# One transfer a pair for the operand and the result of the triangular inverses, GLA sample values read from 16 copies, and a host order that counts eight transfers under way

## The chip, the cores and the metric

One core of a Trainium2 chip runs the whole program. The core has a tensor engine for matrix products (PE; PEld is its weight load), a vector engine (DVE), a scalar engine (ACT), a general engine (POOL) and a sync engine (SP) that here issues every transfer between the chip's memory and the on-chip buffers (SBUF). Products land in PSUM banks. The metric is the device time of one execution in microseconds; lower is better.

## The reference

One step of a decoder layer for 1024 prompt tokens and 8 sample tokens, model width 1024, all in fp32. The weights are the same for both groups.

```python
p = jnp.einsum('btd,dn->btn', x, w_in)                 # 1024 -> 9360 columns
# GLA, 4 heads: S_t = diag(a_t) S_{t-1} + k_t^T v_t ; o_t = q_t S_t
# RWKV-7, 16 heads of 64:
#   S_t = S_{t-1} (diag(w_t) - kk_t^T (kk_t * a_t)) + v_t^T k_t ; y_t = S_t r_t
m = (jax.nn.sigmoid(gate_a) * jnp.einsum('btc,cd->btd', o_gla, w_up_gla)
     + jax.nn.sigmoid(gate_b) * jnp.einsum('btc,cd->btd', o_rwkv, w_up_rwkv))
out = jnp.einsum('btd,de->bte', m, w_out)
y_out = _layernorm(DEEPNORM_ALPHA * x + out, ln_g, ln_b, LN_EPS)
```

The outputs are the layer's result for both groups and the new states of both recurrences.

## The kernel before

**Passes.** The tokens go through in two passes of 512; the first carries the 8 sample tokens as well. In each pass the input projection runs in blocks of 128 output columns. A block is 24 products for each piece of tokens: eight slices of the model width, and three products each, because weights and tokens are split into a high and a low part (`wpart`, `xh`, `xl`) and the product of the two low parts is left out. The blocks come in a fixed plan (`make_plan`): for each of eight pairs of RWKV heads the rows r, k, v and the output gate, between them the rows of the four GLA heads, and then as many blocks of the merge gates as the list `GATES` gives to that pair. After both passes come the two up projections, the output projection and the normalization.

**A pair of RWKV heads.** `front` makes decays and products for 8 chunks of 64 tokens. Each chunk and head needs the inverse of a 64x64 unit triangular matrix. Its two 32x32 diagonal blocks are inverted on POOL, in 31 steps of a multiply (`Xt`) and an add (`X`). For that the blocks go through the chip's memory: four stores write them to `LD`; four loads of 128 KB (line 1281) bring the same 32 partitions' worth of operand into each quarter of the partitions of `L_` (tile `wide`), since each quarter q holds every fourth column group of the inverses. After POOL, four stores of 32 KB (line 1303) write the inverses from `X` to `XD`, and loads bring them back as `XT` and `Yd`. `back` then transposes a part of `XT` on DVE into `Xd` and forms the off-diagonal block with two small groups of products on PE (`Xd` by `Ld`, then `Yd` by `Xt`). `turn`, `chain` (eight dependent steps of three products on the bank `pch`) and `norm` follow. The buffers of a pair come back when its chain has ended.

**GLA samples.** For each of the four heads `gla_sample` stores the eight sample rows of values to `vd` (line 1040), and for two sample tokens at a time loads them into all 128 partitions (line 1049), next to the state of those tokens.

**The order.** Work is written as generators, one a stream. On the host, `run` keeps a clock for each engine and always emits the operation with the smallest key: its start by the clocks, less a priority of its kind (`PRIO`, for PE `FOR_PE`). Each engine then runs its list strictly in that order; operations that two engines can do go to the one that ends first by these clocks (`start`). A transfer is priced by `transfer` from its packets; the clock `dma` is one queue for all transfers. `AGE` weighs changes of ACT's function table, `BIAS` and `ASIDE` the choice between engines, `URGENT` the weights when PE has none ahead. `AHEAD` is how many blocks ahead the loads of the next tokens' operand (x) start, `RAWS` how many rows of it may be loaded ahead of their casts.

SP issues transfers one after another. The framework gives the transfers a small ring of semaphores: each transfer reuses the one of the transfer eight before it, and SP waits until that one has landed.

Of the kernel before, what the change touches and what calls it, by code (L numbers as in the profile page):

```python
# [10 lines left out]
F32 = mybir.dt.float32  # L11
# [9 lines left out]
P = 128  # L21
# [3 lines left out]
NS = 8  # L25
# [4 lines left out]
GH, GDK, GDV = 4, 128, 256  # L30
# [25 lines left out]
BANKS = {"proj": 2, "big": 5, "pch": 1}  # L56

KEEP = 0
AHEAD = 6

RAWS = 5


WARM = 9
# [3 lines left out]
LEAD = 2  # L68
SPARE_ROWS = 10
EARLY_GATES = 16  # L70
GATES = [[3, 1, 3, 1, 2, 3, 2, 1], [2, 1, 3, 5, 0, 1, 4, 0]]


HOP = {"P": 0.2, "D": 0.418, "G": 0.115, "V": 0.064, "A": 0.14}

AFTER = {"A": 0.13, "V": 0.13, "G": 0.147, "S": 0.13}
SWITCH = 0.092
HOLD = 0.11
TABLE = 1.28

AGE = 1.487

SPARE = 0.411
LANDED = 0.648
BIAS = 0.148
ASIDE = 1.497

PRIO = {"evacuate": 0.383, "pair": 0.309, "turn": 0.598, "chain": 0.413, "norm": 0.266, "x": 0.754,
        "lora": 0.377, "rank": 1.051, "head": 0.246, "gate": -0.174, "w": 0.3, "out": 0.424, "state": 0.186,
        "block": 0.718}  # L90
FOR_PE = {"pair": 1.47, "turn": 1.208, "chain": 0.733, "norm": 1.48, "lora": 1.838, "rank": 2.757,
          "head": 0.983, "gate": 2.698, "state": 2.188, "out": 0}
STAND, SCARCE, PER_ROW = 0.033, 0.043, 0.107

URGENT = 1.952
SIGMOID, EXP = "sigmoid_and_others", "natural_log_exp_and_others"
SETS = {AF.Sigmoid: SIGMOID, AF.Tanh: SIGMOID, AF.Exp: EXP, AF.Ln: EXP}

# [119 lines left out]
def transfer(out, src):  # L218

    n = 4 * min(run_of(out), run_of(src), 512 if src.tensor.space == out.tensor.space else 1024)  # L220
    packets = out.nbytes() / n
    slow = 2.2 if any(int(s) == 0 and int(m) > 1 for s, m in src.ap) else 1.45 if packets <= 32 and n > 2048 else 1.0
    if out.tensor.space == DRAM:
        return packets * (0.01 + n * 4.2e-5) / 16, 1.2
    return slow * packets * (0.01 + n * 4.65e-5) / 16, 1.7
# [46 lines left out]
class Order:  # L272
# [4 lines left out]
    def __init__(self, nc):  # L277
        self.P, self.A, self.V, self.G, self.S, self.E, self.C = (Engine(**e) for e in (
            {"P": nc.tensor}, {"A": nc.scalar}, {"V": nc.vector}, {"G": nc.gpsimd}, {"S": nc.sync},
            {"V": nc.vector, "G": nc.gpsimd}, {"A": nc.scalar, "V": nc.vector}))  # L280
        self.tiles = (P, P)
        self.quads = {"V": {}, "A": {}}
        self.time = dict.fromkeys("PAVGS", 0.0)
        self.port = dict.fromkeys("VG", 0.0)
        self.dma = 0.0
        self.table = EXP
        self.ready, self.read = {}, {}
        self.streams = []
        self.idle, self.make, self.home, self.wait = {}, {}, {}, {}
        self.kept, self.tile = {}, {}  # L290
# [65 lines left out]
    def start(self, op):  # L356

        best = None
        for eng, fn, cost in op.ways:
            free, t = self.time[eng] + (SWITCH if eng == "P" and op.tiles != self.tiles else 0.0), 0.0  # L360
            for x in (*op.outs, *op.ins):
                at, by = self.ready.get(x.tensor.name, (0.0, None))
                if eng == "S" and by == "D" and x is op.out:
                    continue
                if by != eng:
                    at += HOP.get(by, 0.0) + (SPARE if eng == "P" and by in ("V", "A", "G") else LANDED if by == "D" else 0.0)
                elif eng != "P" and x is not op.out:
                    at += AFTER[eng]
                t = max(t, at)
            t = max(t, *(self.read.get(x.tensor.name, 0.0) for x in (*op.outs, *(y for y in op.ins if y.space == PSUM))))  # L370
            if eng in op.port:
                free = max(free, self.port["G" if eng == "V" else "V"])
            late, t = free - t, max(t, free)
            if eng in "VA" and self.held(eng, op):
                cost += HOLD
            end = t + cost
            if len(op.ways) > 1:
                end += BIAS if eng == "V" and "A" in op.ways[0][0] else ASIDE if eng == "G" and "G" in op.port else 0.0
            if best is None or end < best[0]:
                best = end, t  # L380
                op.eng, op.fn, op.cost, op.late = eng, fn, cost, max(0.0, late)
        return best[1]
# [10 lines left out]
    def run(self):  # L393
        while self.streams:
            best, before = None, list(self.streams)
            self.urgent = self.needed()
            stand = max(STAND, SCARCE - PER_ROW * len(self.idle["row"]))
            for s in before:
                self.advance(s)
                if s.op is not None:  # L400
                    t = self.start(s.op)
                    if s.op.eng == "P":
                        key = t - stand * s.for_pe - (SWITCH if s.op.tiles != self.tiles else 0.0)
                    else:
                        key = t - s.prio
                    if s.kind in self.urgent:
                        key -= URGENT
                    if s.op.table not in (None, self.table):
                        key += max(0.0, TABLE - AGE * s.op.late)
                    if best is None or key < best[0]:  # L410
                        best = key, t, s
            if best is None:
                assert self.streams != before, "streams wait for one another"
                continue
            _, t, s = best
            op, s.op = s.op, None
            cost = op.cost
            if op.table not in (None, self.table):
                cost += TABLE
                self.table = op.table  # L420
                self.nc.scalar.preload_act_table_set(self.table)  # L421
            op.fn()
            self.time[op.eng] = max(self.time[op.eng], t + cost)
            if op.eng in op.port:
                self.port[op.eng] = t + cost
            if op.eng == "P":
                self.tiles = op.tiles
            elif op.eng in "VA":
                for x, q in self.starts(op):
                    self.quads[op.eng][x is op.out, x.space] = q  # L430
            end = t + cost
            if op.eng == "S":
                self.dma = max(self.dma, end) + op.lag[0]
                end = self.dma + op.lag[1]
            for x in op.outs:
                n = x.tensor.name
                self.ready[n] = max(end, self.ready.get(n, (0.0,))[0]), "D" if op.eng == "S" else op.eng
            for x in op.ins:
                n = x.tensor.name
                self.read[n] = max(self.read.get(n, 0.0), end)  # L440


class Kern(Order):
# [586 lines left out]
    def gla_sample(self, h, q, k, v, al, bufs):  # L1030
# [5 lines left out]
        vs = vs_[:NS]  # L1036
        yield A.copy(vs, pv_)
        self.free(pv_)
        vd = self.dr.tile([NS, GDV], F32, name=f"vd{h}")
        yield self.S.dma_start(vd, vs)  # L1040
        self.free(vs_)
        W = 2

        def load(n):
            Sg, vb = bufs[n % 2]
            b = slice(n * W, n * W + W)
            yield self.S.dma_start(Sg[:, :W * GDV].rearrange("p (b v) -> p b v", b=W),
                                   a["state_gla"][0, b, h].rearrange("b k v -> k b v"))
            yield self.S.dma_start(vb[:, :W * GDV], vd[b].rearrange("b v -> (b v)").partition_broadcast(P))
        yield from load(0)  # L1050
        yield from load(1)
        po = yield from self.bank("big", [P, 2, GDV])
# [1 line left out]
        for g in range(2):  # L1054
            for n in (2 * g, 2 * g + 1):
                Sg, vb = (x[:, :W * GDV].rearrange("p (b v) -> p b v", b=W) for x in bufs[n % 2])
                for w in range(W):
                    t = HT + n * W + w
# [129 lines left out]
    def front(self, c, p, st, d):  # L1188
        a, A, V, E = self.a, self.A, self.V, self.E
        BK_, L_ = yield from self.get("wide", 2)  # L1190
# [14 lines left out]
        r, kb, v = (x[:, :HT] for x in st)  # L1205
# [51 lines left out]
        for n, y in enumerate(p4):  # L1257
            x, h = H * (n // 2), n % 2
# [3 lines left out]
        NU = 4 * NCH  # L1262
        LD = self.dr.tile([4, NCH, 32, 32], F32, name=f"LD{c.i}{p}")
        for q in range(2):
            b = slice(32 * q, 32 * q + 32)
# [4 lines left out]
        for h in range(2):  # L1270
            for n in range(2):
                g = 2 * h + n
# [3 lines left out]
        X = X_.rearrange("p (i t) -> p i t", t=32)  # L1276
        yield E.memset(X, 0.0)
        for q in range(4):
            yield E.memset(X_[NU * q:NU * q + NU, q::36], 1.0)
        for q in range(4):  # L1280
            yield self.S.dma_start(L_[NU * q:NU * q + NU, :32 * 32], LD.rearrange("n c s t -> (n c) (s t)"))
        BT = self.dr.tile([P, NCH * P], F32, name=f"BT{c.i}{p}")
        for f in range(2):
            y = yield from self.row(HT)
# [5 lines left out]
        for j in range(31):  # L1290
# [5 lines left out]
            if j % 5 == 4 and j < 20:  # L1296
                b = j // 5
# [1 line left out]
        self.free(tm)  # L1299
        XT = (yield from self.get("XT")).rearrange("p (c h t) -> p c h t", c=NCH, h=2)  # L1300
        XD = self.dr.tile([4 * NCH, 32, 32], F32, name=f"XD{c.i}{p}")
        for q in range(4):
            yield self.S.dma_start(XD.rearrange("u (i g) t -> g u i t", g=4)[q], X[NU * q:NU * q + NU])
        self.free(X_)

        Yd_ = yield from self.get("Yd")
# [603 lines left out]
```

## Time and profile before

| | us |
|---|---|
| median of 3 runs | 1439.07 (1438.75 to 1439.47) |
| the profiled execution | 1439.84 |
| its span, first to last instruction | 1438.0 |
| PE busy | 1420.8 |
| DVE busy | 1054.8 |
| ACT busy | 834.2 |
| POOL busy | 412.6 |

In the profile, "out<-in" names what an instruction writes and reads by the program's tiles; nearly every instruction has line 239, the line of the helper that emits it, so tiles tell the places. "x8" counts instructions of a group. Idle time has behind it what ended it. SPq is the sync engine's queue of transfer issues.

### The profile page before, as it was taken

How to read it: one execution, taken by the hardware profiler on the slowest of the kernel's cores; microseconds unless marked ns; L12 is line 12 of the kernel's file. 1: busy time of each engine (PE TensorE's matmuls, PEld its weight loads, DVE VectorE, ACT ScalarE, POOL GpSimd, SP SyncE). 2: the span in 40 equal slices, each digit the busy share in tenths (PEclk: the TensorE clock that was granted, in tenths of full speed). 3: DMA queues.
4: the chain of work that ended last, by engine and by line, in shares of the span. 5: the costliest groups of instructions: out<-in, count | busy, mean ns of one | idle time of the engine just before them, and what ended most of it. 6: DMA issues, size and time to landing. Idle time of an engine off the chain costs nothing.

```text
span 1438.0 us, 30397 instructions
## 1 busy us (share of the span) xinstructions
PE 1420.8 (99%) x10640; PEld 1250.2 (87%) x10640; DVE 1054.8 (73%) x2137; ACT 834.2 (58%) x2074; POOL 412.6 (29%) x1148
## 2 busy tenths in 40 slices
PE   9999999999999999999999999999999999999997
PEld 9999999999999998787878787887888898897786
DVE  6778566978586988558665978889867865666685
ACT  6656757666758675546455646565657664654210
POOL 1050506260525251533414352253423150000000
PEclk9999999999999999999999999999999999999999
DMA  9896889686888786886688677567578578699832
GB/s 323 267 299 204 283 287 312 218 299 224 281 276 279 268 263 210 244 250 180 187 241 253 189 197 228 172 188 249 151 233 238 175 223 264 210 293 318 279 123 84
DMA packets 284788, 340.12 MB, mean 237 GB/s; under 512 B 159027, under 2 KB 174524, under 8 KB 284636
## 3 DMA queue, kind: packets, MB, share of 16 engines
q1 hardware_dynamic: 284636, 338.18, 75.2%
q8 instruction: 85, 1.39, 0.4%
q14 instruction: 67, 0.55, 0.1%
HBM read 210.03 MB, written 127.00 MB: 234 GB/s over the span
## 4 chain that ended last, share of the span: by engine, by line
PE 81%; DVE 7%; ACT 4%; DMA 3%; issue 2%; POOL 2%; SPq 1%; DVEq 0%; ACTq 0%; POOLq 0%
PE proj L239 52%; PE big L239 24%; PE pch L239 5%; DVE row L239 3%; ACT row L239 3%; SPq L239 1%; DVE wide L239 1%; DVE gg L239 1%; POOL Xt L239 1%; POOL X L239 1%; DMA row<-o_rwkv 1%; DVE wpart L239 1%; ACT L421 1%; ACT wpart L239 1%; DMA XT<-XD 0%
## 5 line engine op out<-in xcount | busy, mean ns | idle before, releaser
L239 PE MATMUL proj<-xh,wpart 128*128 128x256 f32 (+3 forms) x3712 | 905.3, 328 | 2.9 <-DVE wpart L239 1.4
L239 PEld LDWEIGHTS proj<-xh,wpart 128*128 128x128 f32 x3712 | 618.5, 188 | 56.3 <-issue 7.3
L239 PE MATMUL proj<-xl,wpart 128*128 128x512 f32 (+3 forms) x1856 | 606.7, 327 | 0.0
L239 PEld LDWEIGHTS proj<-xl,wpart 128*128 128x128 f32 x1856 | 349.7, 188 | 25.1 <-issue 3.1
L239 POOL TENSOR_TENSOR Xt<-X,wide 128x60 f32<-128x60 f32 (+24 forms) x496 | 172.0, 347 | 399.5 <-DMA wide<-LD 292.9
L239 DVE TENSOR_TENSOR wpart<-wraw,wpart 128x512 fp32r<-128x512 f32 x210 | 145.5, 700 | 68.5 <-ACT wpart L239 63.7
L239 POOL TENSOR_TENSOR X<-X,Xt 128x60 f32<-128x60 f32 (+24 forms) x496 | 179.4, 362 | 38.5
L239 DVE TENSOR_TENSOR row<-row 128x512 f32<-128x512 f32 (+9 forms) x340 | 173.5, 525 | 13.6 <-ACT row L239 6.8
L239 ACT CAST wpart<-wraw 128x512 fp32r<-128x512 f32 x210 | 128.8, 619 | 84.4 <-PE proj L239 39.0
L239 ACT ACTIVATE row<-row 128x512 f32<-128x512 f32 (+5 forms) x229 | 137.9, 611 | 6.5 <-DVE row L239 2.7
L239 PE MATMUL big<-xh,wpart 128*128 128x256 f32 (+3 forms) x560 | 132.5, 324 | 0.3 <-ACT xh L239 0.3
L239 POOL TENSOR_TENSOR row<-row 128x512 f32<-128x512 f32 (+3 forms) x29 | 37.5, 1302 | 279.4 <-DVE row L239 162.1
L239 ACT COPY row<-big 64x256 f32<-64x256 f32 (+6 forms) x188 | 63.4, 350 | 73.0 <-PE big L239 67.1
L239 DVE TENSOR_TENSOR wide<-pch,gg 64x65 f32<-64x65 f32 x224 | 49.8, 222 | 75.4 <-PE pch L239 73.0
L239 PEld LDWEIGHTS big<-xh,wpart 128*128 128x128 f32 x560 | 93.5, 189 | 8.4 <-ACT xh L239 0.8
L239 ACT COPY rh<-pch 128x130 f32<-128x130 f32 x125 | 33.5, 268 | 103.9 <-PE pch L239 103.3
L239 PE MATMUL big<-xl,wpart 128*128 128x256 f32 (+3 forms) x280 | 90.2, 322 | 0.5 <-DVE xl L239 0.5
L239 DVE SCALAR_TENSOR_TENSOR row<-proj,pv,row 128x255 f32<-128x255 f32 (+1 forms) x95 | 54.5, 574 | 44.1 <-ACT tail L239 26.1
L239 ACT COPY wide<-pch 64x65 f32<-64x65 f32 x237 | 49.3, 208 | 48.9 <-PE pch L239 45.7
L421 ACT ACT_TABLE_LOAD x60 | 77.0, 1283 | 1.0
L239 PE MATMUL big<-row 128*64 128x64 f32 (+5 forms) x680 | 68.6, 287 | 0.3 <-ACT row L239 0.3
L239 ACT ACTIVATE row<-proj,omu 128x256 f32<-128x256 f32 (+1 forms) x95 | 51.7, 545 | 24.7 <-PE proj L239 23.9
(219 smaller groups left out, 2035.4 us busy)
## 6 DMA issues: line engine op xcount, KB each, us to landing
w<-wpart SPq DMA_DIRECT2D x146, 512.0 KB
wpart<-w SPq DMA_DIRECT2D x146, 512.0 KB
wraw<-w_in SPq DMA_DIRECT2D x146, 256.0 KB
wide<-LD SPq DMA_DIRECT2D x64, 128.0 KB
BT<-row SPq DMA_DIRECT2D x32, 256.0 KB
wide<-BT SPq DMA_DIRECT2D x64, 128.0 KB
wraw<-w_up_gla SPq DMA_DIRECT2D x32, 256.0 KB
row<-w_out SPq DMA_DIRECT2D x32, 256.0 KB
```

Of the source, the lines that this page charges most:

```text
L239: ways.append((eng, lambda call=call: call(out, *args, **kw), price(eng, name, out, args, ins)))
L421: self.nc.scalar.preload_act_table_set(self.table)
```

## The change

The operand of the inverses is loaded by one transfer that reads `LD` four times over, and the inverses are stored by one transfer. The sample values are stored to `vd` sixteen times, and each load reads each copy into eight partitions. In the host's order a transfer may not start before the eighth transfer back has ended by the clocks, less 0.3 us; a repeated source counts as slow only above eight repeats. Eight numbers of the order, two tables of weights and the dealing of the gate blocks are new.

```diff
-AHEAD = 6
+AHEAD = 4
-RAWS = 5
+RAWS = 6
-GATES = [[3, 1, 3, 1, 2, 3, 2, 1], [2, 1, 3, 5, 0, 1, 4, 0]]
+GATES = [[4, 1, 2, 0, 1, 4, 4, 0], [3, 0, 3, 6, 0, 1, 3, 0]]
+FLIGHT, EARLY = 8, 0.3
-AGE = 1.487
+AGE = 1.077
-BIAS = 0.148
-ASIDE = 1.497
+BIAS = 0.149
+ASIDE = 1.951
-PRIO = {"evacuate": 0.383, "pair": 0.309, "turn": 0.598, "chain": 0.413, "norm": 0.266, "x": 0.754,
-        "lora": 0.377, "rank": 1.051, "head": 0.246, "gate": -0.174, "w": 0.3, "out": 0.424, "state": 0.186,
-        "block": 0.718}
-FOR_PE = {"pair": 1.47, "turn": 1.208, "chain": 0.733, "norm": 1.48, "lora": 1.838, "rank": 2.757,
-          "head": 0.983, "gate": 2.698, "state": 2.188, "out": 0}
-STAND, SCARCE, PER_ROW = 0.033, 0.043, 0.107
-URGENT = 1.952
+PRIO = {"evacuate": 0.383, "pair": 0.309, "turn": 0.53, "chain": 0.3, "norm": 0.242, "x": 0.645,
+        "lora": 0.207, "rank": 0.674, "head": 0.199, "gate": 0.131, "w": 0.3, "out": 0.52, "state": 0.151,
+        "block": 1.599}
+FOR_PE = {"pair": 1.84, "turn": 1.151, "chain": 0.476, "norm": 1.207, "lora": 3.885, "rank": 2.504,
+          "head": 0.199, "gate": 2.37, "state": 1.781, "out": 0.03}
+STAND, SCARCE, PER_ROW = 0.013, 0.026, 0.104
+URGENT = 2.707
...
-    slow = 2.2 if any(int(s) == 0 and int(m) > 1 for s, m in src.ap) else 1.45 if packets <= 32 and n > 2048 else 1.0
+    slow = 2.2 if any(int(s) == 0 and int(m) > 8 for s, m in src.ap) else 1.45 if packets <= 32 and n > 2048 else 1.0
...
+        self.flight = [0.0] * FLIGHT
...
+            if eng == "S":
+                t = max(t, self.flight[-FLIGHT])
...
                 end = self.dma + op.lag[1]
+                self.flight.append(end - EARLY)
...
-        vd = self.dr.tile([NS, GDV], F32, name=f"vd{h}")
-        yield self.S.dma_start(vd, vs)
+        vd = self.dr.tile([16, NS * GDV], F32, name=f"vd{h}")
+        yield self.S.dma_start(vd.rearrange("c (b v) -> b c v", b=NS), vs.unsqueeze(1).to_broadcast([NS, 16, GDV]))
...
-            yield self.S.dma_start(vb[:, :W * GDV], vd[b].rearrange("b v -> (b v)").partition_broadcast(P))
+            yield self.S.dma_start(vb[:, :W * GDV],
+                                   vd[:, n * W * GDV:(n + 1) * W * GDV].unsqueeze(0).to_broadcast([P // 16, 16, W * GDV]))
...
-        for q in range(4):
-            yield self.S.dma_start(L_[NU * q:NU * q + NU, :32 * 32], LD.rearrange("n c s t -> (n c) (s t)"))
+        yield self.S.dma_start(L_[:, :32 * 32],
+                               LD.rearrange("n c s t -> (n c) (s t)").unsqueeze(0).to_broadcast([4, NU, 32 * 32]))
...
-        for q in range(4):
-            yield self.S.dma_start(XD.rearrange("u (i g) t -> g u i t", g=4)[q], X[NU * q:NU * q + NU])
+        yield self.S.dma_start(XD.rearrange("u (i g) t -> g u i t", g=4), X)
```

## The prediction

> **What bounds the kernel now.** I read the page first, then the busy time by stretch, then what TensorE waited for, then one such wait in the order of time. From the page: the span, the engines, the chain that ended last, and one of the two groups of the 32x32 inverses on POOL.
>
> ```profile
> span 1438.0 us, 30397 instructions
> PE 1420.8 (99%) x10640; PEld 1250.2 (87%) x10640; DVE 1054.8 (73%) x2137; ACT 834.2 (58%) x2074; POOL 412.6 (29%) x1148
> PE 81%; DVE 7%; ACT 4%; DMA 3%; issue 2%; POOL 2%; SPq 1%; DVEq 0%; ACTq 0%; POOLq 0%
> L239 POOL TENSOR_TENSOR Xt<-X,wide 128x60 f32<-128x60 f32 (+24 forms) x496 | 172.0, 347 | 399.5 <-DMA wide<-LD 292.9
> ```
>
> TensorE (PE) is busy for 1420.8 of 1438.0 us and carries 81% of the last chain. It is idle for 17.2 us in all. POOL waits 292.9 us for the load that this change merges, but POOL is busy only 29% of the span, and most of that wait is POOL standing ready long before the next pair of heads arrives. A big wait on a spare engine is not a big gain. The next view gives the busy time in some stretches (columns: stretch, length, then PE, PEld, DVE, ACT, POOL, clock, DMA share, GB/s).
>
> ```profile
> 108.00:180.00 72.00, 70.60 (x647) 68.52 (x646) 48.69 (x95) 47.84 (x126) 22.48 (x71) 1.00 0.78 245
> 252.00:324.00 72.00, 69.20 (x666) 66.52 (x665) 59.59 (x125) 50.03 (x130) 29.80 (x76) 1.00 0.78 257
> 396.00:468.00 72.00, 70.70 (x647) 67.83 (x646) 52.25 (x103) 50.23 (x129) 26.20 (x73) 1.00 0.84 275
> 1430.40:1438.00 7.60, 0.04 (x1) 0.00 (x0) 4.38 (x9) 0.50 (x2) 0.00 (x0) 0.70 0.19 69
> ```
>
> The last 7.6 us are the end of the program: PE has finished, DVE normalizes the last rows and they are stored. The three stretches, all in the first pass over the tokens, lose 1.4, 2.8 and 1.3 us, 5.5 together. What ended PE's waits (columns: total us, times, longest):
>
> ```profile
> PE pch L239 <- DVE wide L239: 1.8, 4, 1.2
> PE proj L239 <- DVE wpart L239: 1.4, 1, 1.4
> PE proj L239 <- DVE row L239: 1.3, 1, 1.3
> PE pch L544 <- DVE warm L541: 1.1, 1, 1.1
> PE big L239 <- ACT part L239: 0.9, 1, 0.9
> ```
>
> 1.1 us is the start, before the first warm-up product. So 17.2 - 7.6 - 1.1 = 8.5 us is idle time in the middle, in single waits of at most 1.4 us behind DVE or ACT. None names a transfer, but one hides one. Around 296 us the timeline (start, length, engine, what, idle before it) shows:
>
> ```profile
> 294.75 0.62 ACT L239 CAST wpart<-wraw 128x512 fp32r<-128x512 f32 x1 [1.65 <-DMA w<-wpart]
> 295.40 0.69 DVE L239 TENSOR_TENSOR wpart<-wraw,wpart 128x512 fp32r<-128x512 f32 x1 [2.22 <-ACT wpart L239]
> 295.96 0.62 ACT L239 CAST wpart<-wraw 128x512 fp32r<-128x512 f32 x1 [0.59 <-DMA w<-wpart]
> 296.61 0.46 PE L239 MATMUL pch<-wide,gg 128*128 128x130 f32 x2 [1.19 <-DVE wide L239]
> ```
>
> ACT stands for 1.65 us until the store of a weight block has landed and its buffer is free; DVE has the subtraction of that block ahead of the state update, and PE waits 1.19 us for the update. Here the host-written order had expected a transfer sooner than it came.
>
> **The change, part by part.** No product on PE is added or dropped, so the 1420.8 us stay, apart from what a new sequence of shapes does. Three costs remain: SP's issues, the length of the inverse's way through the queues, and the order itself.
>
> *Issues.* Issue times on SP (min/median/max ns):
>
> ```profile
> L239 SPq DMA_DIRECT2D wide<-LD x64: 303/421/916, 63.9 to 1141.9; - x64
> L239 SPq DMA_DIRECT2D XD<-X x64: 549/607/1572, 99.1 to 1182.1; - x64
> SPq L239 <- PE proj L239: 183.9, 96, 5.6
> ```
>
> Each of the 16 pairs loses three loads and three stores: 3 x 0.421 + 3 x 0.607 = 3.1 us of SP, 49 us over the kernel. SP waits 183.9 us for PE alone (buffers that matmuls still read), so this mostly turns into more waiting: worth nothing by itself. It also frees six of the places that the new order counts.
>
> *The operand's load.* The first pair, in order of time:
>
> ```profile
> 63.90 1.85 SPq L239 DMA_DIRECT2D wide<-LD  x4
> 68.22 0.33 POOL L239 TENSOR_TENSOR Xt<-X,wide 128x31 f32<-128x31 f32 x1 [63.24 <-DMA wide<-LD]
> 96.43 0.21 POOL L239 TENSOR_TENSOR X<-X,Xt 128x8 f32<-128x8 f32 x1
> 99.08 0.58 SPq L239 DMA_DIRECT2D XD<-X  x1
> 108.49 0.83 SPq L239 DMA_DIRECT2D XT<-XD  x2
> 111.29 0.93 SPq L239 DMA_DIRECT2D XT<-XD  x2
> 119.11 1.24 DVE L239 STREAM_TRANSPOSE Xd<-XT 32x128 f32<-32x128 f32 x4
> 120.63 0.43 PE L239 MATMUL big<-Xd,Ld 128*32 128x128 f32 x8
> 63.90:68.20 4.30, 4.30 (x38) 4.30 (x38) 2.46 (x4) 4.11 (x10) 0.00 (x0) 1.00 0.77 221
> ```
>
> From the first issue to POOL's start are 68.22 - 63.90 = 4.3 us. In that stretch (last row) the engines were 77% busy at 221 GB/s, so all sixteen would move 221 / 0.77 = 287 GB/s. A 128 KB load needs 0.46 us of data; from the end of the last issue (65.75) to POOL's start are 2.47 us, so about 2.0 us are landing. One load of 512 KB: 0.42 issue + 2.0 landing + 1.83 data = 4.25 us if it spreads over all sixteen engines, a gain of 0.1. No row shows how a copy with only four copies outermost is spread; if it ran on four engines its data would take 4 x 1.83 = 7.3 us and the whole 9.7, a loss of 5.4.
>
> *The store of the inverse.* It saves 1.8 us of issues; its 128 KB take 0.46 us at that rate, or 1.8 on four engines, so it comes out between -1.8 and -0.4 us. The 128-byte pieces may go slower than that rate; the same factor would then lie on both sides. Load and store together move the inverse's result by -1.9 to +5.0 us.
>
> What covers that? In the first pair POOL ends at 96.64 and the store is issued at 99.08, 2.4 us later; the last read-back is issued by 112.22, and with 2.5 us of landing is there at 114.7, while DVE takes it up at 119.11, 4.4 us later. Slack 6.8 us. The tightest case I looked at is the seventh pair:
>
> ```profile
> 525.02 0.27 POOL L239 TENSOR_TENSOR X<-X,Xt 128x8 f32<-128x8 f32 x1
> 525.32 3.51 SPq L239 DMA_DIRECT2D XD<-X  x4
> 533.77 0.92 SPq L239 DMA_DIRECT2D XT<-XD  x2
> 542.36 0.94 DVE L239 STREAM_TRANSPOSE Xd<-XT 32x128 f32<-32x128 f32 x3
> ```
>
> There POOL's end and the store touch, and 534.69 + 2.5 to 542.36 leaves 5.2 us. So slack of 5.2 to 6.8 us, PE's filler of projection blocks meanwhile, covers both ends in the slots of before; I charge 0. Without that cover the next to be late would be the product on Xd (at 120.63, 0.3 us behind its transposes), and behind it everything in PE's queue.
>
> The Trainium skill ("DMA: Bandwidth & Descriptors", section "Why a DMA increments its semaphore by 16 and not by 1") says a copy runs on the largest number of engines up to sixteen that divides the slowest dimension of both its sides, and "Rules for kernel authors" on that page names a leading repeat of c copies as confining it to c. By that rule load and store run on four engines and the slow ends hold; no run here shows it yet. It is a rule against this change, and its result is the second rival.
>
> *GLA values.* The store of the eight sample rows grows from 8 to 128 KB, four times in the kernel: 0.4 us more data at 287 GB/s on sixteen engines, 1.8 if on four. The loads read the same amount.
>
> ```profile
> ACT row L239 <- DMA row<-vd: 0.7, 1, 0.7
> ```
>
> ACT waited 0.7 us for them in all, while PE ran blocks: 0, bounds -0.7 to +1.8 a head.
>
> *Loads of x.* They start four blocks ahead instead of six, with up to six rows loaded ahead of their casts instead of five.
>
> ```profile
> 1289.94 5.00 DMA row<-o_rwkv
> 1380.22 5.58 PE big L239 x24
> ```
>
> A block of 24 products 512 wide takes 5.58 us, so four are 22 us, against 5.0 us for the load that the last chain shows. Cost 0; the cover would have to shrink fourfold.
>
> *The order.* Everything else is the host's list: a limit of eight transfers under way, new weights, and gate blocks dealt to other pairs. It can only touch the 8.5 us in the middle, from below by creating waits. Gain between 0 and 8.5; I take half, 4.25, because four waits (1.4, 1.3, 1.2 and 0.9 us) hold over half of it, the three stretches that lose most have a DMA share of 0.78 to 0.84, and the one I followed hangs on a transfer expected too soon, which is what the new limit describes.
>
> **The sum.** The profiled execution took 1439.84 us, 1438.0 of span and 1.8 around it, and stood 0.8 above the median of 1439.07. 1439.84 - 4.25 - 0.8 = **1434.8 us**, with 1420.8 busy, 1.1 start and 7.6 tail unchanged.
>
> **The rivals.** *The waits only move: 1439.* For it: of those four waits I saw a transfer behind one only, and each ends with DVE or ACT; a list order corrected in one place is late in another. Also here: the merged copies could be taken apart again below the program, and then nothing but the order changes. Against it: the first pass alone leaves 5.5 us to win.
>
> *The inverse comes late and PE stands in its queue: 1449, slower.* The operand's load runs on four engines. The order books it at the full rate, 1.9 us sooner than before, while it comes 5.0 us later: 6.9 us of error against slack of 5.2 to 6.8, 0.1 to 1.7 us on PE a pair, 0.9 x 16 = 14 us on top of 1434.8. It decides from about 5 us of lateness on. Weight blocks queued behind the long load on the same engines would add to it. For it: PE's queue is strict, and 120.63 follows its transposes at once. Against it: the slack, and that PE has blocks to run until then.
>
> **How the numbers follow.** Forecast 0.48, waits only move 0.27, late inverse 0.25. About 0.2%, 2.9 us, is what a measurement tells from no change: 1436.2 to 1441.9. The forecast lies below that band, the first rival in it, the second above, so faster 0.48, same 0.27, slower 0.25. All of the middle gone is 1430.6; waits too short to appear as idle, since the recorded ends of matmuls overlap, may give a few us more: low end 1427. High end the late inverse, 1449. The forecast's own range is 1430 to 1436.
>
> **What would show it.** Right: PE idle between start and tail falls from 8.5 to about 4 us, PE busy stays near 1421. Load: POOL's first product 4 us after the issue means sixteen engines, 9 to 10 means four. If it is late and harmless, the product on Xd follows its transposes without a new wait on PE. If PE's waits name Xd, Xt or wpart 16 times, the late inverse has won. If PE's busy time moves by more than 3 us, the sequence of shapes mattered, and my sum lacks a term.

## The result: 8.5% slower

The changed kernel took **1560.08 us** (1558.21 to 1566.03) against 1439.27 of the kernel before, a ratio of 1.0845 (95% interval 1.0816 to 1.0875). The prediction said 1434.8 us with a range of 1427 to 1449. The time lies 111 us above the range, and the kernel became slower where the forecast had it faster.

The page of the profile after has these lines for the span, the engines and the inverses' products on POOL (in the last line, after the bar: busy, mean ns, idle before and what ended it).

```profile
span 1564.2 us, 30246 instructions
PE 1460.5 (93%) x10640; PEld 1282.2 (82%) x10640; DVE 1067.6 (68%) x2179; ACT 822.4 (53%) x2050; POOL 374.0 (24%) x1122
L240 POOL TENSOR_TENSOR Xt<-X,wide 128x60 f32<-128x60 f32 (+24 forms) x496 | 170.4, 343 | 615.0 <-DMA wide<-LD 542.9
```

The same 10640 products keep PE busy for 1460.5 us instead of 1420.8, 39.7 more. PE is idle for 1564.2 - 1460.5 = 103.7 us instead of 17.2, 86.5 more. Both have to be explained. (The profiled execution is the slowest of the four, so its 126 us exceed the 121 between the medians.) What ended PE's waits, then SP's, then ACT's (total us, times, longest):

```profile
PE proj L240 <- DMA wpart<-w: 44.2, 12, 7.2
PE pch L240 <- ACT rh L240: 19.3, 5, 5.8
PE pch L240 <- DVE wide L240: 14.0, 5, 4.7
```

```profile
SPq L240 <- DMA wide<-LD: 86.7, 14, 7.7
```

```profile
ACT wpart L240 <- DMA w<-wpart: 28.4, 10, 7.1
```

PE hardly waits for the inverse itself: nothing for `Xd`, and once 0.5 us for `Xt`. It waits for weight blocks (`wpart<-w`), and for the small state copies (`rh`, `wide`) that ACT and DVE make. SP stands 14 times, in 16 pairs, until the merged load has landed. In the first pair (start, length, then the operation and the idle time before it) it takes 74.40 - 63.78 = 10.6 us from the issue to POOL, against 4.3 before. Over all sixteen pairs it is 10.1 to 13.5 us, 11.7 in the mean, against 4.2 to 7.0 and 5.1 in the mean before:

```profile
63.78 0.61 SPq L240 DMA_DIRECT2D wide<-LD  x1
...
74.40 0.24 POOL L240 TENSOR_TENSOR Xt<-X,wide 128x31 f32<-128x31 f32 x1 [69.42 <-DMA wide<-LD]
```

One pair of the second pass shows the whole mechanism in order of time:

```profile
845.82 0.60 SPq L240 DMA_DIRECT2D wide<-LD  x1
846.48 0.45 SPq L240 DMA_DIRECT2D wpart<-w  x1
846.98 0.52 SPq L240 DMA_DIRECT2D BT<-row  x1
...
847.54 0.43 SPq L240 DMA_DIRECT2D sg<-row  x1
...
848.01 0.52 SPq L240 DMA_DIRECT2D wide<-Sp  x1
...
848.63 0.54 SPq L240 DMA_DIRECT2D BT<-row  x1
...
849.21 0.50 SPq L240 DMA_DIRECT2D wide<-Sp  x1
...
849.81 8.72 SPq L240 DMA_DIRECT2D wpart<-w  x2
...
851.36 0.63 PE L240 MATMUL proj<-xh,wpart 128*128 128x512 f32 x2
...
858.30 0.24 POOL L240 TENSOR_TENSOR Xt<-X,wide 128x31 f32<-128x31 f32 x1 [32.99 <-DMA wide<-LD]
859.30 0.33 SPq L240 DMA_DIRECT2D row<-state_rwkv  x1
859.41 0.77 PE L240 MATMUL proj<-xh,wpart 128*128 128x512 f32 x1 [6.96 <-DMA wpart<-w]
860.40 1.06 PE L240 MATMUL proj<-xh,wpart 128*128 128x512 f32 x2
```

The load is issued at 845.82, a weight block right behind it at 846.48. The first issue at 849.81 is the eighth transfer, the load counted. The next one reuses the load's place and stands until the load has landed, so these two issues span 8.72 us. POOL sees the load at 858.30. The block that PE needs lands 1.1 us after it. It must be one of those issued at 846.48 and at 849.81, since the last one was issued at 858.5 only and 512 KB took at least 3.5 us to land (in a run below). So it was under way for 9.6 us or more. The tenth issue, at 859.30, reuses the place of the block of 846.48, which points to that block and to 12.8 us. PE, out of blocks, stands for 6.96 us. And then it is slow: two products 512 wide take 1.06 us where they took 0.63. The busy time by stretch (stretch, length, PE, PEld, DVE, ACT, POOL, granted clock, DMA share, GB/s) says why:

```profile
842.00:852.00 10.00, 10.00 (x47) 8.21 (x46) 8.59 (x23) 4.70 (x13) 0.00 (x0) 1.00 0.62 138
852.50:855.00 2.50, 0.00 (x0) 0.00 (x0) 1.03 (x2) 0.58 (x1) 0.00 (x0) 1.00 1.06 260
855.00:859.40 4.40, 0.00 (x0) 0.02 (x1) 0.00 (x0) 0.00 (x0) 0.86 (x4) 0.50 0.45 112
859.40:865.20 5.80, 5.79 (x15) 4.69 (x16) 0.00 (x0) 1.57 (x5) 4.65 (x17) 0.50 0.93 288
865.30:870.00 4.70, 4.70 (x26) 3.97 (x25) 2.65 (x6) 3.46 (x9) 3.92 (x11) 1.00 0.98 270
```

The granted clock falls 2.5 us into the pause and is 0.50 until 5.8 us after it. A pause of 7 us is paid again in slower products; over the kernel 39.7 us of them stand beside 86.5 us of added idle, and the mean granted clock is 0.963 instead of 0.998. The Trainium skill ("TensorE: Matmul & The Clock Gate", "Part 1: The HAM clock gate") states that an idle window of some 3.4 us sets the clock to one half. These rows agree on the half, but here 2.5 us of idle were enough.

PE's second kind of wait, for `rh`, is a step longer. In order of time:

```profile
229.14 0.62 ACT L240 CAST wpart<-wraw 128x512 fp32r<-128x512 f32 x1 [6.41 <-DMA w<-wpart]
...
230.39 0.80 PE L240 MATMUL pch<-rh,XT 128*128 128x130 f32 x2 [4.59 <-ACT rh L240]
```

ACT stood 6.41 us until the store of a weight block had landed. The state copy is behind that cast in ACT's list, and PE stands 4.59 us for it.

### The profile page after: what moved, and what is told of

Read it like the earlier page. It is cut to its first block, busy times and chain, and to the rows that moved or that the text cites. A ratio compares the mean times of both kernels' runs of the same rounds, so it can differ in the third digit from the quotient of the medians.

```text
span 1564.2 us, 30246 instructions
## 1 busy us (share of the span) xinstructions
PE 1460.5 (93%) x10640; PEld 1282.2 (82%) x10640; DVE 1067.6 (68%) x2179; ACT 822.4 (53%) x2050; POOL 374.0 (24%) x1122
## 3 DMA queue, kind: packets, MB, share of 16 engines
q1 hardware_dynamic: 283068, 338.66, 71.4%
## 5 line engine op out<-in xcount | busy, mean ns | idle before, releaser
L240 PE MATMUL proj<-xh,wpart 128*128 128x512 f32 (+3 forms) x3712 | 931.5, 334 | 46.1 <-DMA wpart<-w 44.2
L240 PEld LDWEIGHTS proj<-xh,wpart 128*128 128x128 f32 x3712 | 636.0, 193 | 106.4 <-DMA wpart<-w 34.0
L240 PE MATMUL proj<-xl,wpart 128*128 128x512 f32 (+3 forms) x1856 | 619.1, 334 | 0.1
L240 PEld LDWEIGHTS proj<-xl,wpart 128*128 128x128 f32 x1856 | 358.9, 193 | 26.7 <-issue 2.7
L240 DVE TENSOR_TENSOR wpart<-wraw,wpart 128x512 fp32r<-128x512 f32 x208 | 142.8, 694 | 101.8 <-ACT wpart L240 98.6
L240 DVE TENSOR_TENSOR row<-row 128x512 f32<-128x512 f32 (+10 forms) x363 | 185.9, 527 | 13.1 <-ACT row L240 7.7
L240 POOL TENSOR_TENSOR X<-X,Xt 128x60 f32<-128x60 f32 (+24 forms) x496 | 172.8, 348 | 38.6
L240 ACT ACTIVATE row<-row 128x520 f32<-128x520 f32 (+5 forms) x229 | 137.9, 610 | 26.1 <-DMA row<-vd 10.8
L240 ACT COPY row<-big 128x128 f32<-128x128 f32 (+7 forms) x182 | 59.4, 346 | 66.5 <-PE big L240 62.1
L240 PE MATMUL pch<-rh,XT 128*128 128x130 f32 x256 | 53.5, 292 | 23.1 <-ACT rh L240 19.3
L240 PEld LDWEIGHTS pch<-rh,XT 128*128 128x128 f32 x256 | 45.6, 200 | 30.3 <-ACT rh L240 21.1
```

The source lines that it names most:

```text
L240: ways.append((eng, lambda call=call: call(out, *args, **kw), price(eng, name, out, args, ins)))
```

## The experiments

The theory that the trace suggests: a copy with four copies outermost runs on four engines; it holds them for about 7 us, and the transfers behind it, more than the inverse, make the price. The rivals are that the inverse itself comes late, that a long or a repeated transfer is slow as such, and that the new order is at fault. In the runs that keep the list of before only the transfers that SP is given are exchanged, or spare work is added where the text says so; each engine's order stays as it was. In those with the lists of after it is the other way round. Each time stands beside runs of the kernel before on the same chip, whose medians lay between 1438.7 and 1439.3 us. The code is shortened: `...` and left-out names of the helper stand for what is unchanged.

### One part at a time, in the order of before

**The load alone.**

```diff
-        for q in range(4):
-            yield self.S.dma_start(L_[NU * q:NU * q + NU, :32 * 32], LD.rearrange("n c s t -> (n c) (s t)"))
+        # in the place of the fourth load; the first three are booked but not issued
+        dma_start(L_[:, :32 * 32], LD.rearrange("n c s t -> (n c) (s t)").unsqueeze(0).to_broadcast([4, NU, 32 * 32]))
```

> The kernel before, every engine's list unchanged, only the four loads of the inverses' operand are issued as the one of the change, in the place of the fourth. Theory (few engines): POOL starts 10 to 12 us after the issue instead of 4 to 5, and the time is 1500 to 1555 us. Rival two (late, but covered by the slack that the prediction counted): POOL late, time 1439 to 1453 us. Rival one (the order): 1439 us.

1522.61 us, ratio 1.0585 (1.057 to 1.0601): +84 us from this edit, with every engine's order unchanged. PE's and SP's waits are of the kinds seen after:

```profile
PE proj L239 <- DMA wpart<-w: 28.8, 9, 6.9
PE pch L239 <- ACT rh L239: 19.1, 6, 4.1
```

```profile
SPq L239 <- DMA wide<-LD: 71.4, 14, 6.6
```

**The store alone** (four stores to `XD` as one, in the place of the fourth).

> The kernel before, every engine's list unchanged, only the four stores of the inverses are issued as one, in the place of the fourth. Theory (few engines): 128 KB on four engines take 2 to 3 us more, less 1.8 us of issues: 1437 to 1455 us. Rival three (the store of small pieces is the costly part): above 1480 us.

1438.79 us, 1.000 (0.999 to 1.0009): nothing.

**The sample values alone** (16 copies in `vd`, and the loads of after).

> The kernel before, every engine's list unchanged, only the sample values go through 16 copies: four stores and sixteen loads in the change's form. Theory (few engines, eight here, and only in the first pass): 1437 to 1447 us. Rival one: 1439 us.

1446.51 us, 1.0054 (1.0036 to 1.0072): +7.5 us. ACT waits for these loads, 0.7 us in all before and 12.2 now:

```profile
ACT row L239 <- DMA row<-vc: 12.2, 5, 4.4
```

### From the other side: the order of after

**Load as four in the lists of after, then load and store as four, then also the old values**, so that only the order is left of the change.

```diff
-        dma_start(L_[:, :32 * 32], LD...to_broadcast([4, NU, 32 * 32]))
+        for q in range(4): dma_start(L_[NU * q:NU * q + NU, :32 * 32], LD.rearrange("n c s t -> (n c) (s t)"))
...
-        dma_start(XD.rearrange("u (i g) t -> g u i t", g=4), X)
+        for q in range(4): dma_start(XD.rearrange("u (i g) t -> g u i t", g=4)[q], X[NU * q:NU * q + NU])
```

> The changed kernel, every engine's list unchanged, but the operand of the inverses is issued as four loads of 32 partitions in the place of the one. Theory (the one load is what costs, in this order as in the old one): 1440 to 1475 us, with POOL 4 to 5 us behind the first issue. Rival one (the new order is bad by itself, as the 1507 us of the order with the old transfers suggests): above 1500 us.

> The kernel of the last run with the store of the inverses as four transfers too. Theory (the store on few engines costs nothing that can be measured, as in the old order): within 5 us of the last run. Rival three (the store counts in this order): 10 us or more below it.

> The lists of after, with the load and the store as four and the sample values from one copy: what is left of the change is the order alone. Theory (the order costs by itself, the values cost 7 us in either order): 1446 to 1451 us. Rival (the order is neutral, and values and forms of transfers interact with it): within 3 us of 1439. A second rival (the values cost nothing in this order): 1455 to 1457 us.

Measured 1458.32, 1455.9 and 1445.33 us; the last is 1.0045 (1.0032 to 1.0059). The chain of differences from 1439.3 is: order +6.1, values +10.6, store +2.4 (the intervals of those two runs overlap, so not told from nothing), load +101.8. These add to the 120.8 us measured.

With the order alone the page reads:

```profile
span 1443.4 us, 30420 instructions
PE 1423.0 (99%) x10640; PEld 1253.1 (87%) x10640; DVE 1067.7 (74%) x2179; ACT 820.7 (57%) x2050; POOL 377.6 (26%) x1122
```

PE is idle for 20.4 us, more than the 17.2 of before. The new order wins nothing of the middle here, though its lists were dealt for the merged transfers.

**A run that did not tell what it was meant to.** The order of after was also made anew for the transfers of before:

> The order of the changed kernel (all its numbers, its gate blocks, its eight transfers under way) with the transfers of before: four loads and four stores a pair, the sample values as before. Theory (the merged copies run on few engines, the order is harmless): within 1428 to 1445 us. Rival one (the new order itself is bad): above 1500 us. The part of the forecast that is left, a better order, would show as 1430 to 1436 us.

1506.93 us, 1.047 (1.0453 to 1.0488), in the range of the rival, a bad order. But the prices of the old transfers make the host deal other lists than those of after, so this is not the change without its transfers. It has a hole of its own late in the second pass: PE is busy for 45.41 of the 72 us from 1188 on, at a clock of 0.72.

The same holds for **the limit of eight alone**, added to the host's clocks of before with the old numbers:

> Before, its own numbers and transfers, with only the limit of eight transfers under way added to the order's clocks; the lists are made anew. If the limit describes the chip better (the 1.65 us by which ACT stood behind a store that came later than the order thought), up to 4 us are gained: 1435 to 1438 us. Rival (numbers fitted without the limit suit other lists): 1440 us or above, up to 1455.

1466.59 us, 1.0195 (1.018 to 1.0211), above both ranges. Lists made anew with numbers fitted to other lists cost 28 us here and 68 us above. Neither run gives the price of the limit, only that it does not help by itself.

### Few engines, or a long or repeated transfer?

**Two copies outermost** (the load as two transfers of 256 KB), **128 different rows** (one load of 512 KB, nothing repeated), and **sixteen copies of eight rows** (one load of 512 KB, repeated):

```diff
+        LD...unsqueeze(0).to_broadcast([2, NU, 32 * 32])        # twice
+        LD16.rearrange("n c s t -> (n c) (s t)")                # 128 rows, once
+        LD...[:8].unsqueeze(0).to_broadcast([16, 8, 32 * 32])   # once
```

> The list of before is kept; of the four loads of the operand the first and third are left out, and the second and fourth each bring two quarters (256 KB with two copies outermost). Theory (few engines: such a copy runs on as many engines as it has copies outermost): each runs on two engines, so the 512 KB take longer than in the merged load in the old order: if both share two engines, POOL starts 17 to 19 us after the first issue, if they fall on different pairs of engines, 10 to 11 us; the time is 1500 to 1620 us. Rival (a long transfer is slow as such, or a repeated source is): halves are shorter, POOL starts 6 to 8 us after the issue and the time is between 1440 and 1490 us.

> The list of before is kept; the operand comes in one load of the same 512 KB, but its source is 128 different rows of one block of the chip's memory, so nothing is repeated and the outermost dimension is 128. Only the first 32 rows are the pair's operand; the other 96 are filled once from the output weights, so three quarters of the inverses are not the real ones. Theory (few engines): on sixteen engines POOL starts 4 to 5 us after the issue and the time is 1436 to 1443 us, although bytes and number of transfers are those of the merged load. Rival (one long transfer holds a place of SP's eight or the queue whatever its form): POOL starts 8 us or more after the issue and the time is 1480 to 1525 us.

> The list of before is kept; the operand comes in one load of 512 KB that reads the first eight rows of the block sixteen times over (source with sixteen copies outermost, repeated). The partitions beyond the eighth get rows of other matrices, so most of the inverses are not the real ones. Theory (it is the four outermost copies: with sixteen there are sixteen engines): POOL starts 4 to 5 us after the issue, the time is 1436 to 1443 us. Rival (a source read again and again is slow): POOL starts 9 us or more after the issue, the time is 1490 us or above.

Measured 1593.75 us (1.1081, 1.1046 to 1.1116), 1438.78 (0.9994, 0.9984 to 1.0003) and 1439.3 (1.0003, 0.9994 to 1.0013). The first pair of each, in this order; the three fences show the issue and POOL's start:

```profile
64.54 1.15 SPq L1289 DMA_DIRECT2D wide<-LD  x2
...
80.25 0.24 POOL L239 TENSOR_TENSOR Xt<-X,wide 128x31 f32<-128x31 f32 x1 [75.27 <-DMA wide<-LD]
```

```profile
65.86 0.44 SPq L1293 DMA_DIRECT2D wide<-LD  x1
...
70.44 0.24 POOL L239 TENSOR_TENSOR Xt<-X,wide 128x31 f32<-128x31 f32 x1 [65.47 <-DMA wide<-LD]
```

```profile
64.86 0.60 SPq L1289 DMA_DIRECT2D wide<-LD  x1
...
70.06 0.24 POOL L239 TENSOR_TENSOR Xt<-X,wide 128x31 f32<-128x31 f32 x1 [65.09 <-DMA wide<-LD]
```

From the issue to POOL: 15.7 us with two copies outermost, 10.6 with four, 5.2 with sixteen copies, 4.6 with 128 rows. The bytes are the same each time, and the sixteen copies are a repeated source as well. The outermost count decides. The Trainium skill ("DMA: Bandwidth & Descriptors", "Why a DMA increments its semaphore by 16 and not by 1") says the same, and these four times agree. The two halves were two transfers and still took 15.7 us. By an estimate from the 287 GB/s of the trace before, 18 GB/s an engine, 512 KB take 14.6 us on two engines and 7.3 on four, so both halves seem to have run on the same two.

**The sample values with sixteen copies outermost** (8 copies in `vd`, each load reads the block of them 16 times; the store still has eight rows outermost):

> The list of before is kept; the sample values are stored eight times and each load reads the block of eight copies sixteen times, so the load has sixteen copies outermost instead of eight; the store has still eight rows outermost and 64 KB instead of 128. Theory (loads of 256 KB on eight engines make the 7.5 us of the values): 1438 to 1442 us. Rival (the repeated reading or the store makes them): 1444 to 1448 us.

1439.08 us, 1.0002 (0.9992 to 1.0012), and ACT's wait falls from 12.2 to 2.1 us:

```profile
ACT row L239 <- DMA row<-vc: 2.1, 3, 1.0
```

So the 7.5 us of the values look like the same thing on eight engines. The store was halved as well, so a share of it is not excluded; ACT's wait names the loads.

### The late inverse, or the traffic?

**The inverse late, no traffic**: spare products of 120 elements a row ahead of each inverse on POOL, 14 and 9 of them.

```diff
+        for _ in range(14):    # 9 in the second run
+            tensor_mul(tv, X[:, 0:4, 0:1].to_broadcast([P, 4, 30]), L[:, 0:1, 1:31].to_broadcast([P, 4, 30]))
```

> The kernel before, every engine's list unchanged, its four loads kept, and POOL does 14 more products of 120 columns ahead of each inverse, 6 us or so, so that the inverse comes as late as with the merged load while the transfers run as before. Theory a (the transfers behind): 1439 to 1452 us. Theory b (the late inverse): 1490 to 1525 us.

> The list and the transfers of before; nine spare products of 120 elements a row ahead of each inverse on POOL, aimed at the 6.3 us by which the merged load came later (14 of them made 10 us). Theory (the slack of 5.2 to 6.8 us a pair covers the lateness; what costs is what stands behind the load): 1439 to 1450 us. Rival (lateness itself is the price): 16 x 3 us or more, 1485 us or above.

The pages' engine lines, 14 products first:

```profile
PE 1436.0 (97%) x10640; PEld 1260.7 (85%) x10640; DVE 1065.7 (72%) x2137; ACT 835.4 (56%) x2074; POOL 547.0 (37%) x1372
```

```profile
PE 1422.6 (98%) x10640; PEld 1250.4 (87%) x10640; DVE 1061.9 (73%) x2137; ACT 834.8 (58%) x2074; POOL 491.4 (34%) x1292
```

Against 412.6 us of POOL before, the delay is (547.0 - 412.6) / 16 = 8.4 us a pair and (491.4 - 412.6) / 16 = 4.9. The times are 1492.86 us (1.0365, 1.0311 to 1.0419) and 1447.39 (1.0062, 1.0044 to 1.0081): 54 us and 8 us. The first lies in the range written for the late inverse, so lateness has a price too. The slack covers 5 us of it nearly and is gone at 8, which fits the 5.2 to 6.8 us of the prediction. The load's 6.3 us lie between the two; on a straight line between them they would cost some 26 us.

What makes 8 us of lateness dear is again SP. In every pair of these two runs SP issues the store of the inverse within 0.2 us of POOL's end. It already stands there, with weight blocks behind the store in its list. The wait bears the name of what POOL writes at that moment, `X` or the `row` or `wide` right behind it. SP's waits and PE's with 14 products:

```profile
SPq L239 <- POOL row L239: 53.7, 9, 9.5
SPq L239 <- POOL X L239: 48.1, 6, 13.4
SPq L239 <- POOL wide L239: 13.5, 2, 7.0
```

```profile
PE proj L239 <- DMA wpart<-w: 14.8, 4, 7.2
```

In the kernel before SP waited 2.2 us for `row` and 2.1 for `X`. With the merged load in the list of before these were 6.2 and 7.3, against 71.4 for the load.

**The traffic, operand in time**: the four loads of before, and behind them a transfer of the same 512 KB with four copies outermost, within the chip's memory, that nobody reads. First issued by SP:

```diff
+        self.nc.sync.dma_start(spare..., LD.rearrange("n c s t -> (n c) (s t)").unsqueeze(0).to_broadcast([4, NU, 32 * 32]))
```

> The kernel before, every engine's list unchanged, its four loads kept, and behind them one more transfer of the same shape as the merged load (source read four times, four copies outermost, 512 KB) into a spare place of the chip's memory that nobody reads. It takes the same engines for as long, but the operand comes in time. Theory a (what costs is that everything queued behind the long transfer on its engines and in SP's eight places comes late): 1490 to 1525 us, PE waiting for weight blocks. Theory b (what costs is that the inverse comes late): 1439 to 1452 us.

1510.72 us, 1.0489 (1.0465 to 1.0514): +72 us. PE's waits, SP's, and the first pair:

```profile
PE pch L239 <- ACT rh L239: 21.4, 7, 4.8
PE proj L239 <- DMA wpart<-w: 14.6, 5, 4.4
```

```profile
SPq L239 <- DMA spare<-LD: 43.7, 14, 4.6
```

```profile
63.97 1.85 SPq L1290 DMA_DIRECT2D wide<-LD  x4
...
68.42 0.24 POOL L239 TENSOR_TENSOR Xt<-X,wide 128x31 f32<-128x31 f32 x1 [63.44 <-DMA wide<-LD]
```

POOL starts 68.42 - 63.97 = 4.45 us after the first issue, against 4.3 before, and most of the price is there. Only the operand is in time, though. SP is behind, and issues the store of the inverse late:

```profile
94.91 0.21 POOL L239 TENSOR_TENSOR X<-X,Xt 128x8 f32<-128x8 f32 x1
...
103.81 0.58 SPq L239 DMA_DIRECT2D XD<-X  x1
```

These are 103.81 - 95.12 = 8.7 us, against 2.4 in the first pair before. Then the same issued by POOL, where it takes none of SP's eight places, with four and, as a control, with sixteen copies outermost:

> The list and the transfers of before; after the four loads POOL issues one more transfer of 512 KB that reads the operand four times (four copies outermost, into a spare place of the chip's memory that nobody reads). It is the spare transfer that cost 71.5 us when SP issued it. Theory (the engines are what is held: weight blocks behind it on the same engines come late whoever issues): 1475 to 1515 us. Rival (SP's eight places are what is held: SP cannot issue while the long transfer is under way): 1438 to 1450 us, no wait of SP for the spare transfer, and weight blocks in time.

> As the run with POOL's spare transfer, but it reads eight rows sixteen times, so sixteen copies are outermost: the control. Theory (few engines): the 512 KB and POOL's issue cost little, 1438 to 1446 us. Rival (the bytes or POOL's issue make the price): as the run with four copies.

1486.45 us (1.032, 1.03 to 1.034) and 1441.98 (1.0025, 1.0015 to 1.0034). For a transfer that POOL issues the trace shows the time to landing (least, median, most), with four and with sixteen copies outermost:

```profile
DMA to landing us min/median/max: 9.0/10.3/11.9
```

```profile
DMA to landing us min/median/max: 3.5/3.9/4.4
```

POOL's issue and the bytes cost 3 us; the four engines cost 44 more, without a place of SP's taken by the long transfer. SP now waits for ordinary transfers that have become late, such as the four small loads of the operand; here with POOL's four copies, then in the kernel before:

```profile
SPq L239 <- DMA wide<-LD: 20.2, 32, 1.6
```

```profile
SPq L239 <- DMA wide<-LD: 0.9, 3, 0.4
```

So a price of 44 us comes without a place of SP's. The other 27 of the 72 us appear only when SP issues it; its places are one reason, but the transfer also stands in another queue then, and these two were not separated.

**Lateness and traffic on one scale.** No run has the traffic with the inverse quite in time. With POOL's four copies POOL starts 8.6 us after the first issue, in the mean of the pairs, against 6.0 in the control. The traces allow one measure for all: the time from the first issue of the operand's load to the first issue of the inverse's store, in the mean of the sixteen pairs.

| run | load to store, us | later than before | slower by, us |
|---|---|---|---|
| before | 34.5 | | |
| spare transfer by POOL, sixteen copies | 34.7 | 0.2 | 3 |
| nine spare products | 37.4 | 2.9 | 8 |
| spare transfer by POOL, four copies | 37.8 | 3.3 | 48 |
| spare transfer by SP | 38.7 | 4.2 | 72 |
| merged load alone | 40.0 | 5.6 | 84 |
| fourteen spare products | 41.3 | 6.8 | 54 |

A lateness of 3.3 us with the traffic costs 48 us, one of 2.9 us without it 8, and one of 6.8 us without it costs less than one of 4.2 with it. So the traffic is a cost of its own. On a straight line between the two runs without traffic, lateness would be some 13 of the 48 us, 23 of the 72 and 39 of the 84. This is an estimate from two points of a curve that bends.

### An order that knows the price

After, with one rule added to the host's price:

```diff
+    first = math.gcd(*(next(int(m) for _, m in x.ap if int(m) > 1) for x in (out, src)))
+    if first < 16:
+        packets *= 16 / first
```

> After, with one rule added to the order's price of a transfer: fewer than sixteen copies outermost on either side take sixteen over that number times as long. The transfers are those of after, the lists are made anew. Theory (the price is the traffic: engines held for 7 us a pair, with wpart behind them): an order that knows it can move little, 1520 to 1565 us. Rival (the order's error makes the price: it expects the load at the full rate): 1445 to 1480 us.

1586.62 us, 1.1029 (1.1013 to 1.1046), above both ranges. SP still waits for the load, 98.4 us in 16 waits of at most 8.5. Telling the order the load's length is no cure by itself. The host's clock holds one queue for all sixteen engines, so it takes the load's length from every transfer behind it and knows no four engines that are held; whether that is the reason was not tried, and the caution on lists made anew holds here as well.

None of the runs beats the kernel before. Merging the four loads gains nothing even in a form that spreads (0.9994 and 1.0003).

## Why the prediction was wrong

**The step that failed** is the sentence "So slack of 5.2 to 6.8 us, ... covers both ends in the slots of before; I charge 0". The prediction had both facts: the load on four engines at 9.7 us (10.6 measured in the first pair, 11.7 in the mean), and the slack, which the delayed inverses roughly confirm. It priced only the transfer's own consumer. The transfers that share its engines and SP's places have no such slack: a weight block that was under way for 9.6 us or more stopped PE for 7 us. The rival named this in one sentence ("Weight blocks queued behind the long load on the same engines would add to it") without a price. The term charged at 0 measured 84 us with the load alone and 102 in the new order. Of the 84, some 26 to 39 us are lateness by the straight lines above, and the rest is put down to what the load holds up. Even the lateness does not act mainly where the prediction looked, at the product on `Xd`. The pair in which "POOL's end and the store touch" was read as one with 5.2 us left; but where they touch, any lateness makes SP stand, with weight blocks behind it.

**The form of the copy.** "No row shows how a copy with only four copies outermost is spread" was true, but the rule was at hand and only widened the range. With it as the likeliest case the forecast would have been slower, which is right, but its size not: the late inverse gave 1449.

**PE busy unchanged at 1420.8** failed by 39.7 us. The reading offered for such a case, another sequence of shapes, is not what happened: with the new lists and the old transfers PE is busy for 1423.0 us. The rows above show the lowered clock after a pause instead, and the mean clock fell from 0.998 to 0.963.

**The order's gain of 4.25 us** did not come: with the old transfers the new lists cost 6.1 us. One wait traced to a transfer expected too soon did not show that the limit removes it.

**The store** was right at 0. **The sample values** were bounded at -0.7 to +1.8 us a head, 7.2 at most for four. The 7.5 us in the old order lie just above that; the mechanism offered, the store on four engines, is not the one that ACT's wait names: the loads with eight copies outermost were passed over with "read the same amount". **Issues worth nothing** was right: the merged loads that spread save three a pair, the merged store the other three, and neither gains anything. **What would show it** partly served: "9 to 10 means four" did, and "wpart" in PE's waits did, though it was put down to the late inverse alone.

**What stays open.** The parts in the old order add to 84 + 7.5 + 0 = 91, with the order 97; the change costs 121. The other 24 us are a joint effect of transfers and new lists, 18 of them with the load; no run separates why. Open too is the exact share of the inverse's lateness in the 84 us; 26 and 39 are two readings of a straight line. Of the spare transfer's 72 us, the 27 that only SP's issue brings are not taken apart.

## What to carry to other kernels

Before merging transfers by a repeated source, look at the outermost count on both sides: what it leaves of sixteen engines sets the length, and here the same bytes took 4.6 us or 15.7. Price a long transfer by what is queued behind it on its engines and on the queue that issues it, not by the slack of its own reader. A store that waits for its data has the same effect on the queue that issues it. To separate a host-made order from the transfers it books, keep the lists and exchange only what is issued; asking the host for a new order changes everything at once.

## What the runs showed of the hardware

- 512 KB took 10.6 us from issue to use with four copies outermost, 15.7 with two and 5.2 with sixteen (first pairs). By an estimate from 287 GB/s over sixteen engines, two transfers with two copies each shared the same two.
- Held engines delay transfers of other queues as well: a long transfer issued by POOL made SP's ordinary loads late and cost 44 us more than the control.
- The clock fell 2.5 us into a pause of PE of 7 us and stayed at 0.50 until 5.8 us after it. A pause of 2.6 us (1077.04 to 1079.67 in the trace after) was followed by 3.4 us at 0.50 as well, from 1080.3 on. In this kernel 86.5 us of added idle came with 39.7 us of slower products, 0.46 us for each.
- 128-byte pieces in a store with four outermost, 128 KB a pair, cost nothing that the run could tell (1.000, 0.999 to 1.0009).
